# Where the rounded activations of a one-core transformer kernel lie in SBUF: pitch 1024 bytes, 64 bytes below the weights modulo 512

## The chip, the cores and the metric

The kernel runs on one core of one Trainium2 chip, as a single launch. The metric is device time in microseconds (us) of that core, as the median of several runs.

## The reference

Two transformer blocks in float32 on 256 tokens of width 1024. What matters here is that nearly all the work is products of a weight matrix with the activations of all tokens:

```python
# first block, 16 meta tokens ahead of the 256 (L = 272)
n = rmsnorm(h, norm_mix);  parts = split(n @ w_in)            # 1024 -> 5840
y_a = mla_branch(...)                                         # attention
y_b = gla_branch(...)                                         # gated linear attention
mix = sigmoid(gate_a) * (y_a @ w_o_mla) + sigmoid(gate_b) * (y_b @ w_o_gla)
h = h + mix @ w_out
# expert stage: 16384 experts, 8 heads, top 16 by product keys
q = rmsnorm(h) @ w_q;  s = q . sub_keys;  idx, gate = top16(...)
act = gelu(sum(h * u_tab[idx]));  h = h + sum(act * gate * v_tab[idx])
# second block
proj = rmsnorm(h) @ w_in_2;  mix = [stick_breaking(...), differential_attention(...)]
h = h + mix @ w_o_2
u = conv3(rmsnorm(h) @ w_up);  h = h + (gelu(gate) * val) @ w_down      # 1024 -> 2 x 2816 -> 1024
h = h + sigmoid(rmsnorm(h) @ w_ple_gate) * (p @ w_ple_proj);  return rmsnorm(h)
```

The expert stage is computed densely: all 16384 experts for all tokens, with a gate that is zero for experts not chosen.

## The kernel before, in words

**Layout.** Activations lie with features on the 128 partitions and tokens along the free dimension. An activation of 1024 features is a tile [128, 8, w]: eight feature chunks k, each a run of w float32 values per partition, w being 256 (T) or 272 (L). The distance from one chunk to the next, the pitch, is thus 1024 or 1088 bytes.

**Weights.** A stream of 352 units, each [128, 1024] float32 (512 KB), is loaded by SP into a few `raw` slots and split by `_split_next` into a rounded part `hi` (ACT copy to the rounded type, line 398) and a rest `lo` = raw - hi (DVE or POOL, line 279). Three pairs of `hi`/`lo` slots come from the pool `wst`; `more_slots` adds one in some stages. A unit holds eight 128x128 blocks of 512 bytes per partition.

**Products.** Activations are split the same way into two tiles, here called the rounded activations: a `hi` and a `lo` one (`xnh`, `xnl`, `xg0`, `xg1`, `mix0`, `mix1`, `ffn0`, `ffn1`, `cb` and so on). One unit is then 24 matmuls of 128x128 weights by 256 tokens: `hi` weights by `hi` activations, `hi` by `lo`, and `lo` by `hi`. In `fm` (lines 349, 350, 352) both sides advance with k and all 24 add up in one PSUM region:

```python
for k in range(kc):
    mm(ps, view(w[0], k), x[0][:, k0 + k, sl], start=first and k == 0, stop=False)   # L349
    mm(ps, view(w[0], k), x[1][:, k0 + k, sl], start=False, stop=False)              # L350
for k in range(kc):
    mm(ps, view(w[1], k), x[0][:, k0 + k, sl], start=False, stop=last and k == kc - 1) # L352
```

In the second half of the expert stage (lines 1270, 1271, 1274, activations `cb`) and in the down projection (lines 1589, 1590, 1593, activations `ffn`) the activation stays and the weight block advances, with eight PSUM regions.

**Stages in order**, with the activation that the 24-matmul units read: norm and input projection (`xnh1`/`xnl1`), gates and attention (the same), `ob` and `oa` (`ybT`, `yaT`), `out` (`mix`), expert queries `pq` (`xg`), the `u` table (128 units, `xnh2`/`xnl2`; beside it selection and, from there on, gate building on DVE and short float32 matmuls of line 1187), the `v` table (128 units, `cb`), the second block's `dv`, `dqk`, `sv`, `sqk` (`xnh3`/`xnl3`), output `o2` (`mx2`), `up` (44 units; `xg4` for the first six, then `xnh4`/`xnl4`), `dn` (22 units, `ffn`), `pp` (`ppn`), `pg` (`xnh5`/`xnl5`).

**What sets the order.** The order on each engine is the order of the program text, with generators that are stepped between units (`tick`). SBUF addresses follow from the order in which tiles are allocated in the pools.

**Names touched.** `new_xn` (the normalized activations; from pool `gp` for n = 1, 2, from `bp` after that), `block1`, `block2`, and the pools `b1`, `b1b`, `xg`, `b2`, `b2a`, `b2f`.

Of the kernel before, what the change touches and what calls it, by code (L numbers as in the profile page):

```python
# [9 lines left out]
F32 = mybir.dt.float32  # L10
F32R = mybir.dt.float32r
# [10 lines left out]
T = 256  # L22
L = 272
NM = 16
KD = 8
# [171 lines left out]
class Kern:  # L197
# [218 lines left out]
    def new_xn(self, n):  # L416

        pool = self.gp if n < 3 else self.bp
        hi = pool.tile([128, KD, L], F32R, tag="xnh", name=f"xnh{n}", bufs=1)
        lo = pool.tile([128, KD, L], F32R, tag="xnl", name=f"xnl{n}", bufs=1)  # L420
        return hi, lo


    def sq_begin(self, pool, bufs=2):
# [75 lines left out]
    def block1(self):  # L500
# [3 lines left out]
        bp = es.enter_context(tc.tile_pool(name="b1", bufs=1))  # L504
        wk = es.enter_context(tc.tile_pool(name="b1w", bufs=2))
        ap = ea.enter_context(tc.tile_pool(name="b1a", bufs=1))
        self.bp, self.ap, self.wk, self.b1 = bp, ap, wk, es

        self.mark("norm1")
        xin = bp.tile([128, KD, L], F32, tag="ta", name="xin")  # L510
        g1 = ap.tile([128, KD], F32, name="g1")
        nc.scalar.dma_start(g1, A["vecs"][:, VEC["norm_mix"][0]:VEC["norm_mix"][0] + KD])
# [20 lines left out]
        xn = self.new_xn(1)  # L533
# [191 lines left out]
        for u in range(8):  # L725
            c, kb = divmod(u, 4)
            w = self.unit()
# [13 lines left out]
            if u < 6:  # L741
                w = self.unit()
# [20 lines left out]
        ea.close()  # L763
        ap = ea.enter_context(tc.tile_pool(name="b1b", bufs=1))
        self.ap = ap
        yaT = [ap.tile([128, 8, T], F32R, name=f"yaT{j}") for j in range(2)]
        ybT = [ap.tile([128, 8, T], F32R, name=f"ybT{j}") for j in range(2)]
        gates = ap.tile([128, 16, T], F32, name="gates")
# [35 lines left out]
        mix = [bp.tile([128, 8, T], F32R, tag="t" + "ab"[j], name=f"mix{j}") for j in range(2)]  # L804
# [15 lines left out]
        xgp = self.xgs.enter_context(tc.tile_pool(name="xg", bufs=1, side="right"))  # L820
        self.xgp = xgp
        xg = [xgp.tile([128, 8, T], F32R, name=f"xg{j}") for j in range(2)]
        self.sq_begin(wk, 3)
        for j in range(8):
            ps = self.ps(f"out{j}", T)
# [489 lines left out]
    def block2(self):  # L1315
# [4 lines left out]
        bp = es.enter_context(tc.tile_pool(name="b2", bufs=1))  # L1320
        wk = es.enter_context(tc.tile_pool(name="b2w", bufs=2))
        ba = ea.enter_context(tc.tile_pool(name="b2a", bufs=1))
        wa = ea.enter_context(tc.tile_pool(name="b2aw", bufs=2))
        self.bp, self.wk = bp, wk
        self.more_slots(bp, 0, 1, len(self.units))

        self.mark("norm3")
        xn = self.new_xn(3)
        self.sq_begin(wk)
        for d in range(KD):  # L1330
            nc.vector.tensor_tensor(h[:, d, :], h[:, d, :], self.acc(d), ALU.add)
# [8 lines left out]
        pneg = ba.tile([128, 128], F32, name="pneg")  # L1340
        tri = ba.tile([128, 128], F32, name="tri")
        mones = ba.tile([128, 128], F32, name="mones")
        pin = bp.tile([128, 2, T], F32, name="pin")
        for t, n in ((past, "c_past"), (pneg, "c_pneg"), (tri, "c_tri"), (pin, "pin")):
            nc.scalar.dma_start(t, A[n])
        nc.vector.memset(mones, -1.0)
# [9 lines left out]
        sq_ = ba.tile([128, 4, T], F32, name="sbq")  # L1356
        dv = ba.tile([128, 2, 512], F32, name="dv")
        sv = ba.tile([128, 2, 512], F32, name="sv")
        mix = [ba.tile([128, 8, T], F32R, name=f"mx2{j}") for j in range(2)]
        R = ba.tile([128, T], F32, name="R3")  # L1360
        tiles = [(slice(0, 128), 128), (slice(128, 256), 128)]

# [147 lines left out]
        for u in range(4):  # L1510
            w = self.unit()
# [4 lines left out]
        self.drain(sb)  # L1516
        self.dump("mix2", mix[0].bitcast(F32))
        self.mark("wo2")
        xg = [bp.tile([128, 8, T], F32R, name=f"xg4{j}") for j in range(2)]
        self.sq_begin(wk)  # L1520
        for u in range(4):
            w = self.unit()
# [10 lines left out]
        bf = ea.enter_context(tc.tile_pool(name="b2f", bufs=1))  # L1533


        self.mark("ffn up")
        ffn = [bf.tile([128, N_FF, T], F32R, name=f"ffn{j}") for j in range(2)]
        R = bf.tile([128, T], F32, name="R4")
        xn = self.new_xn(4)
# [43 lines left out]
        xn = self.new_xn(5)  # L1583
        self.sq_begin(wk)
        for j in range(N_FF - 2):
            w = self.unit()
# [17 lines left out]


        self.mark("ple")
        ppn = [bp.tile([128, 2, T], F32R, name=f"ppn{j}") for j in range(2)]
        self.split(ppn[0], ppn[1], pin)
        ppj = self.gp.tile([128, KD, L], F32, tag="xnl", name="ppj")[:, :, :T]
        for u in range(2):  # L1610
            w = self.unit()
# [82 lines left out]
```

## Time and profile before

| what | value |
|---|---|
| median of 3 runs | 1605.05 us (1603.83 to 1606.43) |
| the profiled execution's own time | 1612.57 us |
| its span, first to last instruction | 1610.7 us |
| PE busy | 1529.1 us (95%), 12026 matmul records |
| DVE busy | 1171.9 us (73%) |
| ACT busy | 822.6 us (51%) |
| POOL busy | 450.1 us (28%) |
| mean granted TensorE clock | 0.976 of full speed |

The profiled execution took 7.5 us more than the median of the runs shown. A matmul's duration in the profile is a modelled one of some 280 ns that overlaps the next matmul; what counts for a stretch of PE is how far apart the starts of two matmuls or of two units are. In the timeline, consecutive instructions of one line are merged into one row with the start of the first.

### The profile page before, as it was taken

The page shows a single profiled execution, that of the slowest core. Times are in us where ns is not written, and L with a number is a line of the kernel's source. Part 1 is how long each engine was busy: PE and PEld are TensorE (multiplying, and loading weights), DVE is VectorE, ACT ScalarE, POOL GpSimd, SP SyncE. Part 2 cuts the span into 40 slices and gives each one's busy share as a digit, 9 for nine tenths or more (in the row PEclk, how much of TensorE's full clock was granted, in tenths as well). Part 3 has the DMA queues.
Part 4 walks back from the last instruction along what each step waited for, and adds up shares of the span by engine and source line. Part 5 has one row for each costly group of instructions (what it writes and reads, how often), then busy time and mean ns, then how long its engine had stood idle before and what let it go on. Part 6 is the DMA issues. An engine that isn't in the chain of part 4 may idle for free. (4 is left out here: it accounts for less than half of the span.)

```text
span 1610.7 us, 30182 instructions
## 1 busy us (share of the span) xinstructions
PE 1529.1 (95%) x12026; PEld 1462.9 (91%) x12026; DVE 1171.9 (73%) x2217; ACT 822.6 (51%) x1231; POOL 450.1 (28%) x301
## 2 busy tenths in 40 slices
PE   8899999999797999999999999989999989899997
PEld 7777788999697999999999999979999878899997
DVE  7899565679997599999845555545556696887647
ACT  5554455454344555554444444444445565666545
POOL 7556101137677211211232000000003333354203
PEclk9999999999898999999999999999999999999999
DMA  6332224565344644444566666666665433366652
GB/s 217 111 105 80 92 96 146 182 197 155 107 148 142 197 143 145 135 141 132 152 189 213 207 196 193 192 166 198 188 190 183 144 118 91 122 195 200 193 172 92
DMA packets 74547, 252.15 MB, mean 157 GB/s; under 512 B 8180, under 2 KB 13718, under 8 KB 74278
## 3 DMA queue, kind: packets, MB, share of 16 engines
q1 hardware_dynamic: 69298, 243.94, 47.7%
q10 hardware_dynamic: 5108, 6.28, 1.6%
q8 instruction: 94, 1.54, 0.4%
q14 instruction: 47, 0.39, 0.1%
HBM read 246.52 MB, written 3.67 MB: 155 GB/s over the span
## 5 line engine op out<-in xcount | busy, mean ns | idle before, releaser
L398 ACT ACTIVATE hi<-raw 128x1024 fp32r<-128x1024 f32 (+1 forms) x463 | 485.4, 1050 | 523.9 <-PE acc L1271 157.2
L279 DVE TENSOR_TENSOR lo<-raw,hi 128x1024 fp32r<-128x1024 f32 (+2 forms) x388 | 502.9, 1297 | 290.5 <-ACT hi L398 287.8
L279 POOL TENSOR_TENSOR lo<-raw,hi 128x1024 fp32r<-128x1024 f32 (+1 forms) x75 | 180.8, 2417 | 490.2 <-ACT hi L398 475.4
L349 PE MATMUL u<-xnh,hi 128*128 128x256 f32 x1024 | 256.2, 289 | 0.0
L350 PE MATMUL u<-xnl,hi 128*128 128x256 f32 x1024 | 251.0, 284 | 0.0
L1270 PE MATMUL acc<-cb,hi 128*128 128x256 f32 x1008 | 239.8, 280 | 6.9 <-ACT cb L398 6.9
L1271 PE MATMUL acc<-cb,hi 128*128 128x256 f32 x1008 | 239.3, 279 | 0.8 <-DVE cb L336 0.8
L1270 PEld LDWEIGHTS acc<-cb,hi 128*128 128x128 f32 x1008 | 190.7, 189 | 7.1 <-ACT cb L398 7.1
L350 PEld LDWEIGHTS u<-xnl,hi 128*128 128x128 f32 x1024 | 196.2, 192 | 0.0
L349 PEld LDWEIGHTS u<-xnh,hi 128*128 128x128 f32 x1024 | 195.5, 191 | 0.0
L1271 PEld LDWEIGHTS acc<-cb,hi 128*128 128x128 f32 x1008 | 190.7, 189 | 1.2 <-DVE cb L336 1.2
L352 PE MATMUL u<-xnh,lo 128*128 128x256 f32 x1024 | 145.5, 286 | 22.0 <-DVE lo L279 22.0
L352 PEld LDWEIGHTS u<-xnh,lo 128*128 128x128 f32 x1024 | 133.5, 193 | 23.0 <-DVE lo L279 23.0
L1230 POOL TENSOR_TENSOR GA<-GA,gel 128x512 f32<-128x512 f32 (+31 forms) x45 | 65.0, 1444 | 267.5 <-ACT gel L398 254.2
L1274 PE MATMUL acc<-cb,lo 128*128 128x256 f32 x1008 | 136.6, 278 | 0.0
L1274 PEld LDWEIGHTS acc<-cb,lo 128*128 128x128 f32 x1008 | 125.3, 188 | 0.0
L1175 DVE TENSOR_SCALAR oha<-iota,pk 128x128 f32<-128x128 f32 x256 | 94.7, 371 | 0.0
L350 PE MATMUL up<-xnl,hi 128*128 128x256 f32 x304 | 74.0, 282 | 1.3 <-DVE xnl L336 1.3
L349 PE MATMUL up<-xnh,hi 128*128 128x256 f32 x304 | 73.2, 281 | 0.0
L1187 PE MATMUL gate<-oha,ohb 128*128 128x128 f32 x512 | 70.1, 277 | 1.6 <-DVE ohb L1176 1.6
L1176 DVE TENSOR_SCALAR ohb<-iota,pk 128x128 f32<-128x128 f32 x256 | 70.5, 276 | 0.0
L1187 PEld LDWEIGHTS gate<-oha,ohb 128*128 128x128 f32 x512 | 63.3, 191 | 3.4 <-DVE ohb L1176 3.0
(507 smaller groups left out, 3225.5 us busy)
## 6 DMA issues: line engine op xcount, KB each, us to landing
raw<-in_u_tab SPq DMA_DIRECT2D x128, 512.0 KB, 3.6
raw<-in_v_tab SPq DMA_DIRECT2D x128, 512.0 KB, 3.6
raw<-in_w_up SPq DMA_DIRECT2D x44, 512.0 KB, 4.1
raw<-in_w_g SPq DMA_DIRECT2D x24, 512.0 KB, 3.3
raw<-in_w_down SPq DMA_DIRECT2D x22, 512.0 KB, 3.7
raw<-in_w_pq SPq DMA_DIRECT2D x16, 512.0 KB, 3.7
raw<-in_w_c SPq DMA_DIRECT2D x13, 512.0 KB, 4.2
raw<-in_w_gv SPq DMA_DIRECT2D x8, 512.0 KB, 3.6
```

The lines of the kernel that those rows point to most:

```text
L279: eng.tensor_tensor(lo[:, a:b], raw[:, a:b], hi[:, a:b].bitcast(F32), ALU.subtract)
L349: mm(ps, view(w[0], k), x[0][:, k0 + k, sl], start=first and k == 0, stop=False)
L350: mm(ps, view(w[0], k), x[1][:, k0 + k, sl], start=False, stop=False)
L352: mm(ps, view(w[1], k), x[0][:, k0 + k, sl], start=False, stop=last and k == kc - 1)
L398: i = self.last_act = self.nc.scalar.activation(out, x, func, **k).ins
L1175: nc.vector.tensor_scalar(a[:, i, :], iota, pk[:, 0, t:t + 1], pk[:, 2, t:t + 1], ALU.is_equal, ALU.mult)
L1176: nc.vector.tensor_scalar(b[:, i, :], iota, pk[:, 1, t:t + 1], None, ALU.is_equal)
L1187: mm(ps[:, 128 * i:128 * i + 128], b[:, i, :], a[:, i, :], start=True, stop=True)
L1230: nc.gpsimd.tensor_tensor(v[:, :, :n], v[:, :, :n], w, ALU.mult)
L1270: mm(av(d), w[0][:, ds], xh, start=c == 0 and d % 2 == 0, stop=False)
L1271: mm(av(d), w[0][:, ds], xl, start=False, stop=False)
L1274: mm(av(d), w[1][:, ds], xh, start=False, stop=False)
```

## The change

Only addresses change. `new_xn` takes a pitch of 1024 bytes for the tiles after the first norm (n = 2 to 5). Tiles named `pad_...`, which nothing writes or reads, are allocated ahead of others in six pools, and the tiles `xg4`, `ppn`, `pin` and `mx2` are allocated earlier, in another order. No instruction is added or removed; on each of the five engines the instructions stand in the same order as before, with the same waits. Only names' running numbers differ, and the addresses.

Address in the partition modulo 512 of the first byte, as the pools lay it; all `hi` and `lo` weight slots are at 192, before and after, and weight blocks are 512 bytes apart:

| activation (hi and lo tile) | stage | before: address, pitch | after: address, pitch |
|---|---|---|---|
| `xnh1`, `xnl1` | projections, gates | 128, 1088 (meta tokens skipped: 192) | the same |
| `ckvn`, `cqn` | attention's projections | 288 and 416, 32; 1088, 1024 | 224 and 352, 480; the same pitch |
| `yaT`, `ybT` | `oa`, `ob` | 256, 1024 | 128, 1024 |
| `mix` | `out` | 192, 1024 | 128, 1024 |
| `xg` | `pq` | 480, 1024 | 128, 1024 |
| `xnh2`, `xnl2` | `u` | 128, 1088 | 128, 1024 |
| `cb` | `v` | 128, 1024 | 128, 1024 |
| `xnh3` to `xnl5` | `dv`, `dqk`, `sv`, `sqk`, `up`, `pg` | 192, 1088 | 128, 1024 |
| `mx2` | `o2` | 192, 1024 | 128, 1024 |
| `xg4` | `up`, first six units | 192, 1024 | 128, 1024 |
| `ffn` | `dn` | 192, 1024 | 128, 1024 |
| `ppn` | `pp` | 192, 1024 | 128, 1024 |

With a pitch of 1088 the address modulo 512 goes up by 64 from each chunk to the next; with 1024 it is the same for all chunks. At 128, an activation begins 64 bytes below a weight block modulo 512.

```diff
--- before.py
+++ after.py
@@ -416,9 +416,15 @@
     def new_xn(self, n):
 
         pool = self.gp if n < 3 else self.bp
-        hi = pool.tile([128, KD, L], F32R, tag="xnh", name=f"xnh{n}", bufs=1)
-        lo = pool.tile([128, KD, L], F32R, tag="xnl", name=f"xnl{n}", bufs=1)
+        w = L if n == 1 else T
+        hi = pool.tile([128, KD, w], F32R, tag="xnh", name=f"xnh{n}", bufs=1)
+        lo = pool.tile([128, KD, w], F32R, tag="xnl", name=f"xnl{n}", bufs=1)
         return hi, lo
+
+    @staticmethod
+    def pad(pool, n, size):
+
+        pool.tile([128, size // 4], F32, name=n)
 
 
     def sq_begin(self, pool, bufs=2):
@@ -507,6 +513,7 @@
         self.bp, self.ap, self.wk, self.b1 = bp, ap, wk, es
 
         self.mark("norm1")
+        self.pad(bp, "pad_b1", 448)
         xin = bp.tile([128, KD, L], F32, tag="ta", name="xin")
         g1 = ap.tile([128, KD], F32, name="g1")
         nc.scalar.dma_start(g1, A["vecs"][:, VEC["norm_mix"][0]:VEC["norm_mix"][0] + KD])
@@ -763,6 +770,7 @@
         ea.close()
         ap = ea.enter_context(tc.tile_pool(name="b1b", bufs=1))
         self.ap = ap
+        self.pad(ap, "pad_b1b", 448)
         yaT = [ap.tile([128, 8, T], F32R, name=f"yaT{j}") for j in range(2)]
         ybT = [ap.tile([128, 8, T], F32R, name=f"ybT{j}") for j in range(2)]
         gates = ap.tile([128, 16, T], F32, name="gates")
@@ -820,6 +828,7 @@
         xgp = self.xgs.enter_context(tc.tile_pool(name="xg", bufs=1, side="right"))
         self.xgp = xgp
         xg = [xgp.tile([128, 8, T], F32R, name=f"xg{j}") for j in range(2)]
+        self.pad(xgp, "pad_xg", 352)
         self.sq_begin(wk, 3)
         for j in range(8):
             ps = self.ps(f"out{j}", T)
@@ -1322,10 +1331,17 @@
         ba = ea.enter_context(tc.tile_pool(name="b2a", bufs=1))
         wa = ea.enter_context(tc.tile_pool(name="b2aw", bufs=2))
         self.bp, self.wk = bp, wk
+        self.pad(bp, "pad_b2", 448)
+        xn = self.new_xn(3)
+        xg = [bp.tile([128, 8, T], F32R, name=f"xg4{j}") for j in range(2)]
+        ppn = [bp.tile([128, 2, T], F32R, name=f"ppn{j}") for j in range(2)]
+        pin = bp.tile([128, 2, T], F32, name="pin")
+        self.pad(bp, "pad_slot", 64)
         self.more_slots(bp, 0, 1, len(self.units))
+        self.pad(ba, "pad_b2a", 448)
+        mix = [ba.tile([128, 8, T], F32R, name=f"mx2{j}") for j in range(2)]
 
         self.mark("norm3")
-        xn = self.new_xn(3)
         self.sq_begin(wk)
         for d in range(KD):
             nc.vector.tensor_tensor(h[:, d, :], h[:, d, :], self.acc(d), ALU.add)
@@ -1340,7 +1356,6 @@
         pneg = ba.tile([128, 128], F32, name="pneg")
         tri = ba.tile([128, 128], F32, name="tri")
         mones = ba.tile([128, 128], F32, name="mones")
-        pin = bp.tile([128, 2, T], F32, name="pin")
         for t, n in ((past, "c_past"), (pneg, "c_pneg"), (tri, "c_tri"), (pin, "pin")):
             nc.scalar.dma_start(t, A[n])
         nc.vector.memset(mones, -1.0)
@@ -1356,7 +1371,6 @@
         sq_ = ba.tile([128, 4, T], F32, name="sbq")
         dv = ba.tile([128, 2, 512], F32, name="dv")
         sv = ba.tile([128, 2, 512], F32, name="sv")
-        mix = [ba.tile([128, 8, T], F32R, name=f"mx2{j}") for j in range(2)]
         R = ba.tile([128, T], F32, name="R3")
         tiles = [(slice(0, 128), 128), (slice(128, 256), 128)]
 
@@ -1516,7 +1530,6 @@
         self.drain(sb)
         self.dump("mix2", mix[0].bitcast(F32))
         self.mark("wo2")
-        xg = [bp.tile([128, 8, T], F32R, name=f"xg4{j}") for j in range(2)]
         self.sq_begin(wk)
         for u in range(4):
             w = self.unit()
@@ -1534,6 +1547,7 @@
 
 
         self.mark("ffn up")
+        self.pad(bf, "pad_b2f", 448)
         ffn = [bf.tile([128, N_FF, T], F32R, name=f"ffn{j}") for j in range(2)]
         R = bf.tile([128, T], F32, name="R4")
         xn = self.new_xn(4)
@@ -1604,7 +1618,6 @@
 
 
         self.mark("ple")
-        ppn = [bp.tile([128, 2, T], F32R, name=f"ppn{j}") for j in range(2)]
         self.split(ppn[0], ppn[1], pin)
         ppj = self.gp.tile([128, KD, L], F32, tag="xnl", name="ppj")[:, :, :T]
         for u in range(2):
```

## Rows read from the trace of the kernel before

**Rows 1.** Page, first part: the span and the busiest engine's line.

```profile
span 1610.7 us, 30182 instructions
...
PE 1529.1 (95%) x12026; PEld 1462.9 (91%) x12026; DVE 1171.9 (73%) x2217; ACT 822.6 (51%) x1231; POOL 450.1 (28%) x301
```

**Rows 2.** Timeline, PE: two x8 rows of L1274 (v), 58 units apart.

```profile
871.32 1.07 PE L1274 MATMUL acc<-cb,lo 128*128 128x256 f32 x8
...
1029.08 1.07 PE L1274 MATMUL acc<-cb,lo 128*128 128x256 f32 x8
```

**Rows 3.** Timeline, PE: the same line later, 49 units apart.

```profile
1083.93 1.10 PE L1274 MATMUL acc<-cb,lo 128*128 128x256 f32 x8
...
1222.44 1.10 PE L1274 MATMUL acc<-cb,lo 128*128 128x256 f32 x8
```

**Rows 4.** Timeline, PE: dn, 15 units apart.

```profile
1510.54 1.12 PE L1593 MATMUL dn<-ffn,lo 128*128 128x256 f32 x8
...
1553.73 1.12 PE L1593 MATMUL dn<-ffn,lo 128*128 128x256 f32 x8
```

**Rows 5.** Timeline, PE: oa, 4 units apart.

```profile
308.21 1.10 PE L352 MATMUL oa<-yaT,lo 128*128 128x256 f32 x8
...
319.52 1.10 PE L352 MATMUL oa<-yaT,lo 128*128 128x256 f32 x8
```

**Rows 6.** Timeline, PE: u, 22 units apart, and up, 31 units apart.

```profile
797.50 1.11 PE L352 MATMUL u<-xnh,lo 128*128 128x256 f32 x8
...
859.84 1.11 PE L352 MATMUL u<-xnh,lo 128*128 128x256 f32 x8
...
1413.93 1.10 PE L352 MATMUL up<-xnh,lo 128*128 128x256 f32 x8
...
1501.97 1.11 PE L352 MATMUL up<-xnh,lo 128*128 128x256 f32 x8
```

**Rows 7.** Timeline, PE: pq, two pairs of neighbouring units.

```profile
363.14 1.10 PE L352 MATMUL pq<-xg,lo 128*128 128x256 f32 x8
...
365.94 1.10 PE L352 MATMUL pq<-xg,lo 128*128 128x256 f32 x8
...
394.89 1.10 PE L352 MATMUL pq<-xg,lo 128*128 128x256 f32 x8
...
397.72 1.11 PE L352 MATMUL pq<-xg,lo 128*128 128x256 f32 x8
```

**Rows 8.** Timeline, PE: the only wait of PE inside the v stage.

```profile
1076.43 0.58 PE L1270 MATMUL acc<-cb,hi 128*128 128x256 f32 x1 [6.93 <-ACT cb L398]
```

**Rows 9.** Windows: stretch, its us, busy of PE, PEld, DVE, ACT, POOL, PEclk, DMA.

```profile
350.00:405.00 55.00, 52.86 (x438) 51.55 (x437) 49.59 (x160) 23.11 (x34) 35.56 (x20) 1.00 0.51 162
405.00:500.00 95.00, 72.72 (x550) 71.68 (x551) 94.86 (x301) 39.20 (x46) 64.84 (x31) 0.88 0.40 130
...
540.00:760.00 220.00, 220.00 (x1885) 220.00 (x1884) 214.74 (x572) 118.26 (x179) 32.32 (x28) 1.00 0.47 145
...
1074.30:1081.00 6.70, 3.81 (x16) 3.52 (x17) 4.82 (x5) 4.21 (x5) 0.00 (x0) 0.50 0.62 153
1228.00:1338.00 110.00, 99.70 (x641) 88.30 (x641) 85.71 (x173) 62.24 (x129) 40.12 (x24) 0.92 0.41 132
...
1371.00:1409.00 38.00, 32.96 (x240) 31.07 (x239) 33.73 (x57) 22.85 (x43) 12.61 (x9) 0.91 0.41 127
1409.00:1505.00 96.00, 96.00 (x814) 96.00 (x813) 76.49 (x117) 62.18 (x105) 47.40 (x26) 1.00 0.62 197
1505.70:1569.00 63.30, 63.30 (x530) 63.30 (x530) 31.41 (x34) 27.37 (x33) 2.56 (x4) 1.00 0.59 183
```

**Rows 10.** Timeline, PE, u with gate building: a unit, eight gate matmuls, the next unit.

```profile
559.58 1.11 PE L352 MATMUL u<-xnh,lo 128*128 128x256 f32 x8
560.52 1.05 PE L1187 MATMUL gate<-oha,ohb 128*128 128x128 f32 x8
...
563.32 1.11 PE L352 MATMUL u<-xnh,lo 128*128 128x256 f32 x8
```

## Prediction, made before the changed kernel had run

> **What bounds the kernel now.** The page comes first: PE is busy for 1529.1 of 1610.7 us [rows 1], so PE's own pace is the first thing to look at. A matmul's duration there is modelled and overlaps the next, so the pace is read from the timeline, as the distance between the starts of like rows. Nearly all work is the same unit of 24 matmuls of 128x128 by 256, and what the reader is to see is that this unit does not always take the same time, though no wait stands in these stretches and the granted clock is full. In the first part of the v stage it takes (1029.08 - 871.32) / 58 = 2.720 us [rows 2], in the second part, with the same tiles and addresses, (1222.44 - 1083.93) / 49 = 2.827 us [rows 3]. In dn it takes 43.19 / 15 = 2.879 us [rows 4], in oa 11.31 / 4 = 2.828 us [rows 5], in u 62.34 / 22 = 2.834 us and in up 88.04 / 31 = 2.840 us [rows 6], in pq 2.80 or 2.83 us [rows 7].
>
> Beside the table of addresses this falls into an order. Activation and weights at the same place modulo 512 (ffn): 2.879. Activation 64 bytes above (yaT): 2.828. 288 above (xg): 2.80 or 2.83. Wandering through all places (pitch 1088: u, up): 2.834 to 2.840. Sixty-four below (cb): 2.720, but also 2.827. The form of the loop is not the cause: dn and v step their weights in the same way and differ by 0.16 us in a unit.
>
> So a place sets which speeds are possible, and something else picks one. In pq both speeds occur at one place [rows 7], and between them PE only ran other work. In v the change of speed follows PE's only wait there, 6.93 us for ACT [rows 8], after which the granted clock was 0.50, the 1.2 GHz level, from 1074.3 to 1081 us [rows 9]; the fast part had begun after a short wait at full clock. I read this as: the speed is drawn anew where PE restarts, and then kept.
>
> **The Trainium skill speaks against this.** Its page "SBUF — State Buffer", section "Who interferes with whom", gives PE two independent read ports, for weights and for the moving side, and says "PE and ACT never wait on anyone". By that the address would be of no account and the time would stay at 1605. The trace does not agree: equal units at full clock are 2.720 to 2.879 us apart [rows 2 to 4].
>
> **The change part by part.** No instruction is added, removed or moved on any engine or queue, and every wait stays; the pads cost nothing, since nothing touches them, and ACT, DVE and POOL still write whole rows. What changes is the place of the activations that PE reads. Each changed unit goes to the place of cb, so to 2.720 or to 2.827 us. Two places of cb's kind were seen, one fast, one slow, so for the likeliest case I take half of the units at each, 2.773 us; all fast and all slow are the bounds. Saved in us as (half; all fast; all slow):
> - ob and oa, 16 units at 2.828: 16 x 0.055 = 0.9; 1.7; 0.
> - out, o2 and dn, 38 units at the place of ffn, 2.879: 38 x 0.106 = 4.0; 6.0; 2.0.
> - pq, 16 units at 2.815 on the mean, PE busy 52.86 of 55 us [rows 9]: 0.7; 1.5; -0.2.
> - u up to 500 us, 22 units: nothing in any case. DVE is busy 94.86 of 95 us there and PE only 72.72 [rows 9]; a faster PE waits longer for DVE.
> - u from 500 to 780 us, 77 units, where each unit is followed by eight gate matmuls and the pair takes 563.32 - 559.58 = 3.74 us [rows 10]. PE is busy all of it, but DVE is next: 214.74 of 220 us [rows 9], so no more than 5.3 us of 220 can be had, 6.7 us of 280. Half is 77 x 0.061 = 4.7, of which I take 4.0, since DVE's slack does not lie where it is wanted and each unit restarts; all fast, capped, 6.7; all slow 77 x 0.007 = 0.5.
> - u from 780 us, 29 units, DVE far from full: 1.8; 3.3; 0.2.
> - v, 128 units: nothing moves, so 0.
> - dv, dqk, sv, sqk, 24 units from 1228 to 1338 us: PE is idle for 10.3 of 110 us [rows 9] and waits for softmax work, and in dv and sv the activation is the stationary side. I take half of 24 x 0.061: 0.7; all fast in full, 2.7; 0.
> - up, first ten units (1371 to 1409 us): DVE's normalization ends last, DVE busy 33.73 of 38 us [rows 9]: nothing.
> - up, 34 units from 1409 us, PE busy 96.00 of 96.00 and DVE 76.49 [rows 9]: 34 x 0.067 = 2.3; 4.1; 0.4.
> - pp and pg, 10 units: 0.7; 1.2; 0.1.
>
> The sums are 15.1, 27.2 and 3.0 us. The covers hold where I use them: at 2.720 us a unit the stream of weights kept up in v, so it will elsewhere, and in up DVE has a fifth of its time left [rows 9].
>
> **From the profiled execution to the median.** That execution took 1612.57 us, 7.5 more than the median of the runs shown. If those runs had all of v at the fast speed, 52 units x 0.107 = 5.6 us of the 7.5 would be that. I can't tell, so I take the savings from the median: 1605.05 - 15.1 = **1590 us**.
>
> **The rivals.**
> - All changed units fast: 1605 - 27 = 1578 us, and 1572 if v's second part is fast too. For it: the fast part of v began after a warm restart, and most changed stages restart warm, after float32 matmuls. Against: pq, at its own place, shows the slower speed after such restarts too.
> - All slow: 1605 - 3 = 1602 us. For it: 2.827 at that place [rows 3] is what oa has at another, so it may be the usual one. Against: 58 units in a row at 2.720.
> - Slower: v loses its fast part. Its speed is drawn at its start, at 866 us, right behind u, and u's addresses change. With everything else slow, 74 units x 0.107 = 7.9 us are lost against 3.0 saved: 1610 us. It is slower from 28 lost units of v on, and beyond what can be measured from 58 on. For it: the draw happens where the change is. Against: v's own addresses, order and waits stay.
> - The place is not the cause and nothing changes: 1605 us. For it: one place with two speeds. It is also what the Trainium skill's page "SBUF — State Buffer" would have. Against: dn and v, one loop, two places, 2.879 and 2.720.
>
> **How the numbers follow.** Half and half 0.43 (1590 us), all fast 0.28 (1578), all slow 0.17 (1602), v slower 0.07 (1610), nothing 0.05 (1605). A measurement of this kernel can tell some 0.2%, 3.2 us, from no change. Faster by more than that: the first two and 0.07 of all slow, where a little is fast after all, 0.78. Within it: the rest of all slow and nothing, 0.15. Slower: 0.07. The range of 1575 to 1605 us leaves out v's loss, some of nothing, and the lower edge of all fast.
>
> **What would show it.** Right: x8 rows of u behind 780 us, of up, out and dn 2.72 us apart in some stretches and 2.83 in others, never 2.88; a change of speed only where PE waited or ran other matmuls; u before 500 us as long as now. All fast or all slow shows in the same rows. Wrong would be dn and out still at 2.88 with the new addresses, a third speed, or a fast PE in u after 500 us whose gain turns into waits for DVE.

## The result and the profile after

The changed kernel takes 1585.83 us (median of 4 runs, 1582.33 to 1589.32) beside 1604.76 us of the kernel before (4 runs, 1603.83 to 1606.43). The ratio is 0.9881, 95% interval 0.9857 to 0.9904: 19 us faster. An execution over 1.5% longer than the fastest of its kernel is left out of the ratios here and below; there is one, of 1599.13 us in experiment 12. The profiled execution of the changed kernel took 1589.32 us. The head of its page, against [rows 1], has the same number of instructions and 27.5 us less of PE:

```profile
span 1587.5 us, 30182 instructions
...
PE 1501.6 (95%) x12026; PEld 1434.5 (90%) x12026; DVE 1173.9 (74%) x2217; ACT 821.8 (52%) x1231; POOL 451.9 (28%) x301
```

The timeline of PE gives the pace of a unit as before, from rows of one line (start, modelled length, both in us). The pairs are, in this order, oa 7 units apart, u (late part) 22, v's first part 58, v's second part 49, up 31, dn 15:

```profile
306.14 1.07 PE L352 MATMUL oa<-yaT,lo 128*128 128x256 f32 x8
...
325.18 1.07 PE L352 MATMUL oa<-yaT,lo 128*128 128x256 f32 x8
...
791.51 1.11 PE L352 MATMUL u<-xnh,lo 128*128 128x256 f32 x8
...
853.70 1.11 PE L352 MATMUL u<-xnh,lo 128*128 128x256 f32 x8
...
867.88 1.07 PE L1283 MATMUL acc<-cb,lo 128*128 128x256 f32 x8
...
1025.64 1.07 PE L1283 MATMUL acc<-cb,lo 128*128 128x256 f32 x8
...
1080.99 1.07 PE L1283 MATMUL acc<-cb,lo 128*128 128x256 f32 x8
...
1214.27 1.07 PE L1283 MATMUL acc<-cb,lo 128*128 128x256 f32 x8
...
1398.50 1.07 PE L352 MATMUL up<-xnh,lo 128*128 128x256 f32 x8
...
1482.82 1.07 PE L352 MATMUL up<-xnh,lo 128*128 128x256 f32 x8
...
1493.70 1.07 PE L1607 MATMUL dn<-ffn,lo 128*128 128x256 f32 x8
...
1534.50 1.07 PE L1607 MATMUL dn<-ffn,lo 128*128 128x256 f32 x8
```

oa stands at 19.04 / 7 = 2.720 us ([rows 5]: 2.828), up at 84.32 / 31 = 2.720 ([rows 6]: 2.840), dn at 40.80 / 15 = 2.720 ([rows 4]: 2.879). The late part of u stands at 62.19 / 22 = 2.827, hardly below its 2.834 of [rows 6]. v is at 2.720 in both parts this time (157.76 / 58 and 133.28 / 49), where the execution before had lost its second part [rows 3]. The eye needs no division: a row of eight with the length 1.07 is a unit of 2.720 us, one with 1.10 or more a slower one.

Stage by stage, from the first matmul of a stage to the first of the next, in the two profiled executions (1612.57 and 1589.32 us, a difference of 23.3):

| stage | before | after | difference |
|---|---|---|---|
| ob and oa | 45.2 | 43.5 | -1.7 |
| out | 23.0 | 21.8 | -1.3 |
| pq | 55.2 | 55.1 | -0.1 |
| u before the gate building | 142.1 | 140.2 | -1.9 |
| u with the gate building | 240.5 | 240.7 | +0.2 |
| u, late part | 76.6 | 76.4 | -0.2 |
| v | 365.4 | 360.3 | -5.1 |
| dv, dqk, sv, sqk | 106.7 | 104.2 | -2.5 |
| o2 | 31.8 | 31.4 | -0.4 |
| up | 135.4 | 130.2 | -5.1 |
| dn | 63.3 | 59.8 | -3.5 |
| pp and pg | 41.7 | 41.2 | -0.4 |

(The attention's projections ahead of ob give the remaining 1.1; differences are taken before rounding.) One row stands out: u with the gate building holds 64 of the moved units and gives nothing in this execution. The windows view of that stretch (us, busy of PE, PEld, DVE, ACT and POOL, clock, DMA) and PE's waits in it:

```profile
543.00:784.00 241.00, 236.84 (x2028) 233.92 (x2027) 240.02 (x630) 124.32 (x190) 41.18 (x31) 1.00 0.45 140
...
PE gate L1196 <- DVE ohb L1185: 4.2, 7, 0.7
```

DVE is busy for 240.02 of 241 us, and PE waits seven times for a one-hot matrix of DVE (a 128x128 comparison from which the gates are built), 4.2 us in all. In the kernel before, the same view has three such waits and 1.6 us.

### The profile page after: what moved, and what is told of

It reads as the page before. It is cut to its first block, busy times and chain, and to the rows that moved or that the text cites. A ratio compares the mean times of both kernels' runs of the same rounds, so it can differ in the third digit from the quotient of the medians.

```text
span 1587.5 us, 30182 instructions
## 1 busy us (share of the span) xinstructions
PE 1501.6 (95%) x12026; PEld 1434.5 (90%) x12026; DVE 1173.9 (74%) x2217; ACT 821.8 (52%) x1231; POOL 451.9 (28%) x301
## 5 line engine op out<-in xcount | busy, mean ns | idle before, releaser
L349 PE MATMUL u<-xnh,hi 128*128 128x256 f32 x1024 | 252.5, 287 | 0.0
L350 PE MATMUL u<-xnl,hi 128*128 128x256 f32 x1024 | 246.3, 281 | 0.0
L1279 PE MATMUL acc<-cb,hi 128*128 128x256 f32 x1008 | 236.3, 277 | 7.1 <-ACT cb L398 7.1
L1280 PE MATMUL acc<-cb,hi 128*128 128x256 f32 x1008 | 236.0, 277 | 0.8 <-DVE cb L336 0.8
L350 PE MATMUL up<-xnl,hi 128*128 128x256 f32 x304 | 70.8, 277 | 0.7 <-DVE xnl L336 0.7
```

What stands on the lines that cost most here:

```text
L1279: mm(av(d), w[0][:, ds], xh, start=c == 0 and d % 2 == 0, stop=False)
L1280: mm(av(d), w[0][:, ds], xl, start=False, stop=False)
```

## The experiments

The theory after the result: the place of the activation against the weights modulo 512 decides which speeds a unit can have; at 64 bytes below, the fast 2.720 is among them; which of the speeds comes is settled where PE is interrupted; and in the gate building DVE takes the gain. Rivals: the pitch alone does it; the absolute place does it, whatever the weights'; the speed belongs to the stage.

**1. The pitch alone.** The kernel before with the first part of the diff only:

```diff
+        w = L if n == 1 else T
-        hi = pool.tile([128, KD, L], F32R, tag="xnh", name=f"xnh{n}", bufs=1)
+        hi = pool.tile([128, KD, w], F32R, tag="xnh", name=f"xnh{n}", bufs=1)
...
```

> The kernel before with the pitch of 1024 bytes alone, no pads and the old order of allocation. Theory (the place of the activation against the weights modulo 512 sets the speeds of a unit): u gets the place of cb and runs at 2.720 or 2.827 us a unit; the second block's xn goes from wandering to the place of ffn, so up goes from 2.840 to 2.880 us a unit, 34 x 0.04 = 1.4 us lost there, and dn, out and oa keep 2.880, 2.880 and 2.828. In all 1600 to 1606 us. Rival (the pitch is what counts, any constant place will do): up as in the changed kernel, 2.720 or 2.827, and some 1590 us.

Measured: 1599.9 us (10 runs) beside 1605.11 (19), ratio 0.9964, 0.9934 to 0.9994. u's tiles, which the pitch alone puts 64 bytes below the weights, came out at 2.72 in the late part. In up, which the pitch alone puts at the weights' own place, two rows 31 units apart are 89.28 us apart, 2.880 us a unit:

```profile
1404.08 1.12 PE L352 MATMUL up<-xnh,lo 128*128 128x256 f32 x8
...
1493.36 1.12 PE L352 MATMUL up<-xnh,lo 128*128 128x256 f32 x8
```

That is dn's speed of before at dn's place of before [rows 4], in another loop. Up took 136.0 us, 0.6 more than before. The pitch by itself is not the cause; it only makes all eight chunks share one place.

**2. The place without the pitch.** The change with `w = L` for all norms.

> The changed kernel with the old pitch of 1088 bytes. Theory: oa, out, o2 and dn, whose pitch was 1024 before, run at 2.720 or 2.827 us a unit; u, up and pg wander through all places at 2.83 to 2.84. Saved against before: dn up to 3.5, ob, oa and out up to 3, o2 0.5, so 1597 to 1602 us. Rival (the pitch counts): no stage gains, 1605 us. Rival (where a tile begins counts): up and u at 2.720 or 2.827, some 1587 us.

Measured: 1595.86 us (10 runs), ratio 0.9954, 0.9917 to 0.9992. oa, ob, out and dn run at 2.72, u and up, whose chunks wander again, at 2.83 to 2.84. Up's pair, 31 units apart, is 87.84 us apart, 2.834:

```profile
1404.00 1.11 PE L352 MATMUL up<-xnh,lo 128*128 128x256 f32 x8
...
1491.84 1.11 PE L352 MATMUL up<-xnh,lo 128*128 128x256 f32 x8
```

Either half alone, by its ratio, gives 6 or 7 of the 19 us. Together they give more than the sum, though the two intervals are too wide to show that by the times; the rows show it in up, whose tiles need both (2.880 and 2.834 us with one half, 2.720 with both).

**3. The weights moved instead.** Before the weight slots stand 64 bytes more, so that the weights lie at 256 and `ffn`, `xnh4` and the rest, shifted with them where they are allocated behind them, at 192; u's and v's activations stay at 128, now 128 below.

```diff
+        self.pad(pool, "pad_w", 64)
```

> The changed kernel with 64 bytes of padding ahead of the weight slots, which moves the weights to 256 modulo 512 and with them all pools behind: oa, out, o2, up, dn go to 192 and stay 64 below the weights; u, v and pq stay at 128, now 128 below. Theory (place against the weights): oa, out, up and dn at 2.720 or 2.827 us a unit as in the changed kernel; u and v at other speeds than these two. Rival (the activation's own address modulo 512): oa, out, up and dn at 2.880, as all did at 192 before; u and v at 2.720 or 2.827.

Measured: 1606.57 us in one run. Up, whose activations now lie at 192, where the weights lay in the change, keeps 84.32 / 31 = 2.720; v, whose own address did not change, goes to 165.18 / 58 = 2.848 and stays there for all 125 units:

```profile
871.56 1.11 PE L1284 MATMUL acc<-cb,lo 128*128 128x256 f32 x8
...
1036.74 1.12 PE L1284 MATMUL acc<-cb,lo 128*128 128x256 f32 x8
...
1415.56 1.07 PE L353 MATMUL up<-xnh,lo 128*128 128x256 f32 x8
...
1499.88 1.07 PE L353 MATMUL up<-xnh,lo 128*128 128x256 f32 x8
```

So it is the distance between the two operands that counts, not the address of either.

**4. The change once more.** No edit.

> The changed kernel once more, nothing altered. Theory (each restart of PE draws the fast or the slow speed): the same two speeds, but some of the long stretches (u behind the gates, the two parts of v, up, dn) at the other speed than in the first profile. Rival (the speed of a stretch belongs to the program): every stretch as in the first profile, u behind the gates 2.827, both parts of v 2.720, up and dn 2.720.

Measured: 1591.73 us. Late u now runs at 59.84 / 22 = 2.720, and v's second part, from PE's wait on, at 132.85 / 47 = 2.827, both the other way round than in the first profile:

```profile
789.82 1.07 PE L352 MATMUL u<-xnh,lo 128*128 128x256 f32 x8
...
849.66 1.07 PE L352 MATMUL u<-xnh,lo 128*128 128x256 f32 x8
...
1082.61 1.11 PE L1283 MATMUL acc<-cb,lo 128*128 128x256 f32 x8
...
1215.46 1.10 PE L1283 MATMUL acc<-cb,lo 128*128 128x256 f32 x8
```

Same program, same addresses: which speed a stretch gets differs from execution to execution. oa, out and dn were at 2.72 in this profile and in all five others of the change and of its versions in 9 to 12; why these never lost it, no run here tells.

**5 and 6. Other distances.** Only the sizes of the pads change, for instance

```diff
-        self.pad(ap, "pad_b1b", 448)
+        self.pad(ap, "pad_b1b", 288)
```

> The changed kernel with other pads, so that each stage lies at a place of its own, pitch 1024: ob and oa 32 bytes below the weights modulo 512, out 128 below, pq 160 below, dqk, sqk, up and pg 96 below, o2 32 below, dn 192 below; u and v stay 64 below. Theory (each place has its own speeds): out shows the 2.85 us a unit that u and v had at 128 below, u and v keep 2.720 and 2.827, and the other places show constant speeds of their own between 2.72 and 2.88. Rival (64 below is special, any other place costs the same): all others at one speed near 2.83.

> As the run before with another set of places: ob and oa 256 below, out 96 below, pq 32 below, dqk, sqk, up and pg 160 below, o2 128 above, dn 32 above. Theory: out repeats what up shows at 96 below in the run before, pq what oa shows at 32 below, up what pq shows at 160 below, whatever the stage; u and v stay at 2.720 and 2.827. Rival (the speed belongs to the stage): out, pq and up do not repeat the other stage's number.

Measured: 1591.18 and 1598.74 us, one run each. Units in us, from rows of eight of the stage, with the distances of the earlier runs beside them:

| activation against weights, modulo 512 | stages | unit |
|---|---|---|
| 64 below | oa, ob, out, up, dn, u, v | 2.720 or 2.827 |
| same place | dn, out before; up, dn in 1 | 2.88 |
| 32 below | oa, ob, o2 in 5; pq in 6 | 2.84 |
| 96 below | up behind its first six units, dqk, pg in 5 | 2.85 |
| 96 below | up's first six units in 5; out in 6 | 2.82 |
| 128 below | out in 5; v in 3 | 2.85 |
| 160 below | pq in 5; up, dqk, pg in 6 | 2.88 |
| 192 below | dn in 5 | 2.83 |
| 256 below | oa, ob in 6 | 2.88 |
| 32 above | dn in 6 | 2.80 |
| 64 above | oa before | 2.83 |
| 128 above | o2 in 6 | 2.85 |
| 288 above | pq before | 2.80 or 2.83 |

The views for two of them, oa 7 units apart, first 32 below (19.88 / 7 = 2.840), then 256 below (20.16 / 7 = 2.880):

```profile
308.07 1.11 PE L352 MATMUL oa<-yaT,lo 128*128 128x256 f32 x8
...
327.95 1.11 PE L352 MATMUL oa<-yaT,lo 128*128 128x256 f32 x8
```

```profile
308.20 1.12 PE L352 MATMUL oa<-yaT,lo 128*128 128x256 f32 x8
...
328.36 1.12 PE L352 MATMUL oa<-yaT,lo 128*128 128x256 f32 x8
```

The same distance gave the same speed in different stages (160 below in pq and up, 32 below in oa and pq), and none but 64 below reached 2.720. One part of the expectation missed: at 96 below, out took 2.82 us and not the 2.85 of most of up. As up's own first six units took 2.82 in experiment 5, two speeds at one place are not peculiar to 64 below. Distances between the tested ones and most of those above were not tried. Nor is 512 bytes shown to be the period: wherever two of the tested distances differ by 256 bytes they share a speed (same place and 256 below, 2.88; 64 above and 192 below, 2.83; 128 above and 128 below, 2.85; 32 above and 288 above, 2.80), so it may be 256. An activation 320 below, which would tell, was not tried.

**7. Interruptions.** The change with a short float32 matmul of 64 columns, which nothing reads, between units, at seven places in late u, four units apart, and twelve times in v: on the engine six of the twelve stand at v's start, the others from 1062 us on:

```diff
+            if n == T and c % 4 == 0:
+                mm(self.ps(f"ru{c}", 64), self.ones, self.ones[:, :64], start=True, stop=True)
...
+            if c % 10 == 9:
+                mm(self.ps(f"rv{c}", 64), self.ones, self.ones[:, :64], start=True, stop=True)
```

> The changed kernel with a short float32 matmul of 64 columns, whose result nobody reads, put between units: in u behind the gates every 8 units, in v every 10 units. Theory (each restart of PE draws the speed, and it is kept between): some of the 12 pieces of v and of the 3 pieces of u run at 2.720 and some at 2.827 us a unit, and the speed changes at the inserted matmuls only. Rival (the speed of a stretch was set by something else, the half-rate clock or the stage): the pieces go on at the speed that the stretch had, one speed for all of v up to PE's wait and one behind it, as in the two profiles of the changed kernel.

Measured: 1605.73 us in one run. In this profile the speed changes only at an insert, a wait or another stage's matmuls. Two inserts in u, the first turning slow units fast, the second turning fast ones slow (2.72 between the rows up to 798.88, then 2.83):

```profile
787.73 1.11 PE L352 MATMUL u<-xnh,lo 128*128 128x256 f32 x8
788.67 0.33 PE L1246 MATMUL ru<-ones 128*128 128x64 f32 x2
790.72 1.07 PE L352 MATMUL u<-xnh,lo 128*128 128x256 f32 x8
...
798.88 1.07 PE L352 MATMUL u<-xnh,lo 128*128 128x256 f32 x8
799.79 0.33 PE L1246 MATMUL ru<-ones 128*128 128x64 f32 x2
801.90 1.10 PE L352 MATMUL u<-xnh,lo 128*128 128x256 f32 x8
```

Behind the seven inserts of u the units are in turn fast, slow, slow, fast, slow, slow, fast, and the single ones from 1099.76 us on in v follow it too. That is no draw. It looks like a hidden position with three values, one of them fast, which a short matmul moves on by one.

**8. The DVE limit, first try.** Eleven of the splits of u's table go from DVE to POOL:

```diff
-        add("u_tab", lambda j: "p" if j < 36 and j % 4 else "v")
+        add("u_tab", lambda j: "p" if (j < 36 and j % 4) or (36 <= j < 100 and j % 6 == 0) else "v")
```

> The changed kernel with 11 of the splits of the u table between its units 36 and 99 on POOL in place of DVE, 11 x 1.22 = 13.4 us less for DVE in the stretch with gate building. Theory (the gain of the faster units there was taken by DVE, whose backlog sets the pace from the 51st of 63 pairs on): the pairs stay at 3.63 and 3.72 us to the end, the stretch goes from 240.7 to some 232 us, and the kernel to 1576 to 1580 us. Rival (the stretch is held by something else, or POOL's reads slow DVE by as much): the stretch stays at 239 to 242 us and the time at some 1586 us.

Measured: 1601.48 us (10 runs), ratio to before 0.9972, 0.994 to 1.0005: most of the change's gain is lost. The windows view of the stretch with the gates shows it 252.7 us long instead of 240.7, with DVE busy throughout:

```profile
543.50:796.20 252.70, 240.75 (x2023) 236.29 (x2024) 252.70 (x623) 124.39 (x190) 53.65 (x41) 0.99 0.43 134
```

Fewer instructions on DVE took longer. The groups of DVE between 560 and 720 us (busy, mean ns) tell why, here with the eleven splits on POOL, and below it the change:

```profile
L1184 DVE TENSOR_SCALAR oha<-iota,pk 128x128 f32<-128x128 f32 x165 | 68.6, 416 | 0.0
L1185 DVE TENSOR_SCALAR ohb<-iota,pk 128x128 f32<-128x128 f32 x165 | 54.5, 330 | 0.0
```

```profile
L1184 DVE TENSOR_SCALAR oha<-iota,pk 128x128 f32<-128x128 f32 x172 | 60.8, 354 | 0.0
...
L1185 DVE TENSOR_SCALAR ohb<-iota,pk 128x128 f32<-128x128 f32 x172 | 49.0, 285 | 0.0
```

The one-hots grew from 354 to 416 and from 285 to 330 ns on the mean while POOL worked beside them. The timeline shows where: beside each of the ten moved splits that fall into the stretch, one one-hot lasts 2.16 to 2.51 us and ends 0.1 us behind the split, here one on POOL and below it the one-hot on DVE:

```profile
592.48 2.39 POOL L279 TENSOR_TENSOR lo<-raw,hi 128x1024 fp32r<-128x1024 f32 x1 [3.16 <-PE gate L1196]
```

```profile
592.51 2.45 DVE L1184 TENSOR_SCALAR oha<-iota,pk 128x128 f32<-128x128 f32 x1
```

Ten times some 2.1 us is more than the 13.4 us of which the move was to spare DVE. That DVE is the limit of the stretch stands; POOL is no place to move its work to.

**9, 11 and 12. The DVE limit, second try.** One in four of the second one-hots is built on ACT:

```diff
+                    if i == 3:
+                        self.act(b[:, i, :], iota, AF.Abs, bias=pk[:, 1, t:t + 1], scale=-1.0)
+                        self.act(b[:, i, :], b[:, i, :], AF.Relu, bias=1.0, scale=-1.0)
+                        continue
```

> The change, with one in four of VectorE's second one-hot matrices of the gate building (64 of 256) built on ScalarE instead (absolute value of the difference to the index, then one minus it, clipped at zero). Theory (in the stretch of u that builds the gates VectorE is the bound: 240.02 us busy of 241 after the change): this takes about 64 x 0.28 = 18 us off VectorE, the pairs of u keep the spacing of 3.63 and 3.72 us to the end of the stretch, the stretch falls from 240.7 to about 232 us, and the kernel stands at 1577 to 1580 us. Rival (ScalarE, which rounds the upper parts in the same stretch, or the matmuls themselves set the end): the stretch stays at 239 to 242 us and the kernel at about 1586, or above it if ScalarE gets late.

Beside it, on the same chip, the change itself:

> The change itself once more, for a time beside the version with ScalarE's one-hots on the same chip. By the two earlier runs of it 1582 to 1592 us; single runs differ by up to some 5 us, as the late part of u (26 units) and the second part of v (53 units) come out at 2.72 or 2.83 us.

Measured: 1584.16 us (6 runs, 1580.06 to 1589.67) with ACT's one-hots, 1585.81 (6 runs, 1581.96 to 1595.75) for the change; ratios to before 0.9892 (0.9845 to 0.9939) and 0.9894 (0.9848 to 0.994). In the profile the stretch is 232.5 us instead of 240.7, as the theory had it; DVE has time over, and the view of PE's waits in it is empty:

```profile
543.00:776.00 233.00, 233.00 (x2030) 233.00 (x2029) 226.87 (x564) 152.68 (x314) 40.28 (x31) 1.00 0.47 145
```

But the medians differ by 1.7 us only. So the same kernel ran again:

> The version with ScalarE's one-hots once more, as its first profile had the stretch of u with the gates at 232.5 us (240.7 and 239.3 in the change) but its median stood only 1.7 us below the change's own. If the first six times were an unlucky draw of the speeds of u and v: the stretch at 231 to 234 us again and a median of 1575 to 1580, some 1.3% below the kernel before of this comparison's chip (ratio 0.985 or less). If the gain of the stretch is given back later or is there in some executions only: the ratio stays at 0.989, and the profile shows the stretch at 239 us or above, or a later stage that takes longer by as much.

Measured: 1579.79 us (6 runs, 1575.47 to 1599.13) beside 1608.09 (11 runs), ratio 0.9843, 0.9794 to 0.9891. The stretch is 232.5 us once more. This is the lowest median of all, and a ratio as the first case expected. Its interval still overlaps with the change's, so the 7 to 8 us are shown for the stretch and not for the whole time. Single runs of one program spread over 7 to 22 us; v's second part (53 units x 0.107 = 5.7 us) and late u (2.9 us), which come out at either speed, are part of that.

**10. An interruption at every unit.** The change with the same short matmul after each late unit of u:

```diff
+                if gated[0] == T:
+                    mm(self.ps(f"ru{c}{j}", 64), self.ones, self.ones[:, :64], start=True, stop=True)
```

> The change, with one short fp32 matmul (64 columns, nothing reads it) after each unit of u once the gates are done (some 26), v untouched. Theory (a hidden phase with three positions, of which one is fast, moved on by one by each such insert): the late units of u go fast, slow, slow in regular turn, at 2.72 and 2.83 us, one in three fast. Rival 1 (each interruption draws anew): fast and slow units without an order, perhaps half and half. Rival 2 (the speed belongs to the stage or the place alone): all units at one speed. The inserts themselves cost a few us.

Measured: 1597.16 us in one run. The rows of eight of late u, with the inserts between them left out:

```profile
793.26 1.07 PE L352 MATMUL u<-xnh,lo 128*128 128x256 f32 x8
...
796.28 1.10 PE L352 MATMUL u<-xnh,lo 128*128 128x256 f32 x8
...
799.33 1.10 PE L352 MATMUL u<-xnh,lo 128*128 128x256 f32 x8
...
802.33 1.07 PE L352 MATMUL u<-xnh,lo 128*128 128x256 f32 x8
```

1.07, 1.10, 1.10, 1.07: fast, slow, slow goes on in this order to the end of the stage at 864 us without an exception. The cycle of three is shown for this kind of insert. With eight gate matmuls between the units the change's timeline has a cycle of two (gate groups 3.63 and 3.72 us apart in turn for some 50 pairs); what the position is, the runs do not show.

## Why the prediction was right, and where it was not

The forecast was 1590 us and the measured median 1585.83; 15.1 us were to be saved, and 19 were. The frame held: two speeds at 64 bytes below, no unit at 2.88 any more, nothing taken from the order of instructions, and a change of speed only at interruptions, but for one in experiment 11 (below). The page "SBUF — State Buffer" of the Trainium skill, section "Who interferes with whom", by which PE's two reads are independent and it never waits, does not agree with experiments 1 to 3: with the same order of instructions and at full clock (a granted 1.00 while up runs in both kernels and in 1 to 3) the unit goes from 2.72 to 2.88 us by the distance of two operands. Whether it is the two reads that meet, or something else that depends on this distance, no run shows.

By the steps of the sum, predicted and measured in the profile:

- ob and oa, 0.9: 1.7. out, o2 and dn, 4.0: 5.2. up, 2.3: 5.1. All three were mis-sized by **half of the units at each speed**. In oa, out and dn all units came fast, in up all 38 behind the first six, and the bound "all fast" was right for them (1.7, 6.0 and 4.1). What up gave beyond it, 1.0, lies in the first ten units, which I had put at nothing because DVE's normalization ends last there.
- o2 alone contradicts "all fast": its blocks without a wait stand at 2.83 in every profile of the change.
- pq, 0.7: 0.1. The units went to 2.72, but PE's waits for POOL's and ACT's splits in the stage grew from 2.5 to 3.6 us. The splits were next, which I had not asked for pq.
- u up to 500 us, nothing: 0.7. u from 500 to 780, 4.0: 1.0, of which 1.2 lies ahead of the gates and -0.2 with them. This is the step that failed, in this execution. I had put eight gate matmuls behind each of 77 units; only 64 have them, from 549 us on. And I had read DVE's slack as 5.3 of 220 us from a window that began 9 us ahead of the gates and ended at 760 [rows 9]. Over the gates alone the kernel before has 2.6 us of it up to 760, and behind that none:

```profile
549.30:760.00 210.70, 210.70 (x1806) 210.70 (x1805) 208.07 (x556) 112.69 (x171) 32.32 (x28) 1.00 0.46 141
760.00:789.90 29.90, 28.27 (x224) 26.54 (x222) 29.90 (x70) 11.90 (x20) 6.93 (x4) 1.00 0.39 124
```

- What took the gain in the change: gate groups follow each other at 3.63 and 3.72 us for some 50 pairs and then at 4.28 on the mean, where before they followed at 3.74 for 57. From there on DVE is late, because some of its one-hots last over 1 us beside products of POOL (the last section has the rows). The profile of the change has nine of these in the stretch, the one before five. The price itself was right where they are few: experiments 1 and 5, with u at the same place, have three, the stretch takes 236.2 us, and the saving is 4.3. With nine of them it takes 240.7 us in experiments 4, 6 and 7 too, and with seven 239.3 in 10 and 11. Experiments 9 and 12, which take 64 one-hots from DVE, have 232.5. The view for experiment 5:

```profile
547.20:783.40 236.20, 234.46 (x2025) 233.13 (x2024) 234.93 (x627) 124.10 (x190) 41.76 (x31) 1.00 0.46 142
```

- u from 780 us, 1.8: 0.2 in this execution, some 3 in that of experiment 4.
- v, 0: 5.1. Nothing moved there, as said. The profiled execution before had lost its second part and this one had not; experiment 4 lost it with the same program. The gain is not the change's, and is part of why 23.3 us between the profiles are 19 between the medians.
- dv, dqk, sv and sqk, 0.7: 2.5, near the bound of 2.7.
- pp and pg, 0.7: 0.4. Their units came fast, but the stretch behind the last of them, to the end of the span, took 0.6 us longer.
- The sum was better than its terms, and that was luck: without v the terms give 16.9 us in the profile against 15.1, but some gave 7.3 us more than forecast and others 5.5 less.
- **"The speed is drawn anew where PE restarts"** was half right. It changes there, but in a fixed cycle for equal interruptions (experiments 7 and 10). As the start differs from one execution to the next (experiment 4), a single profile still looks like a draw.

The rival in which v loses its fast part at its start came true once, in the profile of experiment 11: from 877 us on, behind a pause of some 0.1 us between two matmuls that the view of waits does not list, 66 units run at 2.83, v takes 366.8 us, and that run stands at 1595.75, the slowest of its six. What made the pause is open. V lost time in the profiled execution of the kernel before too [rows 3]; how often either kernel does so, no run tells.

## What to carry to other kernels

When equal units of matmuls take different times at full clock and without waits, put their start-to-start times beside the addresses of both operands modulo 512 bytes: here a distance of 64 bytes and a pitch of 1024 made units some 5.5% shorter than equal addresses (2.720 against 2.879 us), for some unused bytes. Before counting on a faster PE, read the slack of the next engine over the whole stretch, to its last group and not up to a convenient window's edge. And compare stages over several executions, as one profile can show a stretch at either of two speeds.

## What the runs showed that was not expected

A collision of POOL and DVE explains why the stretch of u with the gates is 240.7 us in some executions and 236.2 in others (experiments 1 and 5, with u at the same place). In the change, the timeline of POOL and DVE between 727 and 747 us has three of POOL's products, here the first and the last, and beside each a one-hot of DVE takes 1.07 or 1.16 us instead of the 0.33 of the rows further down:

```profile
727.79 1.82 POOL L1239 TENSOR_TENSOR GA<-GA,gel 128x400 f32<-128x400 f32 x1 [6.08 <-ACT gel L398]
744.49 1.99 POOL L1239 TENSOR_TENSOR GA<-GA,gel 128x432 f32<-128x432 f32 x1 [6.47 <-ACT gel L398]
```

```profile
728.63 1.07 DVE L1184 TENSOR_SCALAR oha<-iota,pk 128x128 f32<-128x128 f32 x1
...
745.40 1.16 DVE L1184 TENSOR_SCALAR oha<-iota,pk 128x128 f32<-128x128 f32 x1
```

Each long one-hot ends 0.1 us after the product (729.70 against 729.61, 746.56 against 746.48). From 713 to 747 us this happens beside all five products. In the profile of experiment 5 the products of that part run on a shifted beat, here one of 2.39 us, and none of the six between 717 and 755 us stretches a one-hot:

```profile
746.57 2.39 POOL L1239 TENSOR_TENSOR GA<-GA,gel 128x432 f32<-128x432 f32 x1 [5.33 <-ACT gel L398]
```

```profile
746.54 0.33 DVE L1184 TENSOR_SCALAR oha<-iota,pk 128x128 f32<-128x128 f32 x1
...
746.99 0.33 DVE L1184 TENSOR_SCALAR oha<-iota,pk 128x128 f32<-128x128 f32 x1
```

Five times some 0.75 us are 3.7 of the 4.5 us between the two stretches. The Trainium skill's page "SBUF — State Buffer", section "Who interferes with whom", says that when DVE runs in a mode that uses two ports, which it counts as open to `tensor_scalar` under conditions, whichever of DVE and POOL issues first holds the ports they share for its whole instruction and that the other blocks; the rows agree, with a one-hot that lasts until POOL is done. In experiment 5 the product starts 0.03 us behind a one-hot, and it is the product that is long, 2.39 us beside 1.99 for the same size in the change. What puts the two on one beat or the other in an execution was not tried.
